# Second feed-forward by seven products of halves, output projection in four chunks of 276 tokens

## The chip, the cores and the metric

One NeuronCore of a Trainium2 chip runs the whole kernel. The metric is the device time of one execution in microseconds (us). TensorE is the engine of matrix products, VectorE and ScalarE work element by element, GpSimd is a slower third one of that kind, and SyncE (SP) issues nearly all DMA transfers.

## What is computed

One layer of a streaming encoder over 1104 tokens (64 of one group, 16 meta tokens and 1024 of the other), model width 1024, inner width 2816, all in float32:

```python
def half_ffn(x, g, wg, wu, wd):
    h = rmsnorm(x, g)
    return x + 0.5 * ((jax.nn.silu(h @ wg) * (h @ wu)) @ wd)
...
        xp = half_ffn(xp, ffn1_norm[l], ffn1_wg[l], ffn1_wu[l], ffn1_wd[l])
...
        xp = xp + jnp.concatenate([gdn_p, mla_p.astype(gdn_p.dtype)], axis=-1) @ w_out[l]
...
        xp = half_ffn(xp, ffn2_norm[l], ffn2_wg[l], ffn2_wu[l], ffn2_wd[l])
...
    y_prompt = rmsnorm(xp[:, N_META:], final_norm)
```

Between the two feed-forwards lie an input projection, gated DeltaNet heads and latent attention heads; their concatenated output goes through `w_out`. The change touches what comes after attention: the output projection, the second feed-forward and the final norm.

## The kernel before

**Products.** Activations lie transposed, features on partitions and tokens along the free axis. Each float32 operand is split into a high part of type fp32r and a low rest (`wh`, `wl` of a weight, `XH`, `XL` or `ih`, `il` of an activation); a product is three passes, high by high, high by low and low by high (`PASSES`, `mm3`). A weight block of 128 rows by 128 columns is held in the array, tokens stream.

**Chunks.** Tokens are cut two ways. `CH` has three chunks of 336, 384 and 384 tokens. The first feed-forward's gate and up products use four chunks of `F` = 276, taken as two pairs.

**First feed-forward (span 24 to some 800 us).** Its gate and up products are made by seven products of halves: of a pair of chunks, one half of the model width each and gate and up of one inner tile, sums and differences are formed (`half_weights`, `third_weights` and `last_weights` for weights, `norm_pair` for activations `s`), multiplied in the order of `STEPS` (P1, P5, P6, P3, P7, P2, P4), each product 4 blocks x 3 passes, and the results added up on VectorE in `sn` tiles. So 84 matmuls do what 96 do plainly. The first `NPL` = 5 inner tiles are made plainly for pair 0 (`plain_steps`), then 17 steps for both pairs, then 5 for pair 1 (`half_steps`). The inner tile `hb` goes to DRAM (`hd`). Then `down` follows as a stage of its own: `inner_loads` brings `hd` back and splits it, `down_loads` loads and splits the weights `wd`, and `down` multiplies two inner tiles at a time for eight row blocks and the three chunks of `CH`.

**Output projection (1456 to 1584 us).** `out_in` loads the attention's output `oT` row block by row block for chunk 0, 1 and 2 of `CH`, `out_split` splits it (odd rows on GpSimd). `out_proj` runs over eight output blocks `m`, first for chunk 0 alone, in part between attention's last matmuls, then for chunks 1 and 2 together, with 8 weight blocks loaded each time. `add_x1` and `after_o` add the residual, `stats` and `norm_chunk` form the norm's factor and the split input of the second feed-forward.

**Second feed-forward (1584 to 2399 us).** `ffn` goes over 22 inner tiles: `gu` multiplies gate and up over all three chunks (8 blocks x 3 passes x 3 chunks each), `silu` and `gated` make the inner tile and split it in SBUF, and `down` for two inner tiles is woven in two tiles later. The last two tiles go chunk by chunk in `order2` = (1, 2, 0), so that the final norm (`resid_final`, `final_chunk`, `final_turn`) of a chunk runs under the next one's products. `final_turn` turns the result back to rows by products with `ident`, and `fy` is the scaled row tile that is stored.

**Order of work.** `Tasks` interleaves generators at build time by a cost model (`Clock`), so each engine's instructions stand in a fixed order in the program; an engine waits in that order. All instructions carry the line of one recording helper (L424), so rows of the trace are told apart by their tile names.

The step of seven products reads:

```python
STEPS = (("P1", "A0", 0, "B"), ("P5", "S0", 3, "D"), ("P6", "S1", 4, "B"), ("P3", "T1", 2, "D"),
         ("P7", "T0", 5, "B"), ("P2", "A1", 1, "E"), ("P4", "B1", 6, "B"))
```

Of the kernel before, what the change touches and what calls it, by code (L numbers as in the profile page):

```python
# [17 lines left out]
P = 128  # L18
# [72 lines left out]
def f32(ap):  # L91
    return ap.bitcast(F32)
# [470 lines left out]
def ffn_weights(wg, wu, wd):  # L563

    v = [w.rearrange("(k p) n -> p k n", p=P) for w in (wg, wu)]
    g, u = [[Weight("w", x[:, :, j * P:(j + 1) * P], 8, P) for j in range(NF)] for x in v]
    d = [Weight("wd", wd[j * P:(j + 1) * P, :].rearrange("p (k n) -> p k n", n=P), 8, P) for j in range(NF)]
    order = [g[0], u[0], g[1], u[1]]
    for j in range(2, NF, 2):
        order += [g[j], u[j], d[j - 2], d[j - 1], g[j + 1], u[j + 1]]  # L570
    return (g, u, d), order + d[-2:]


def ffn(s, X, xs, W, wk, hp, ready, order, after):

    nc, T = s.nc, s.tasks
    V, A = nc.vector, nc.scalar
    wg, wu, wd = W
    sg, hs, fl = {}, {}, Flags()

    def h_tiles(j):
        hs[j] = tuple(hp.tile([P, T_], F32R, tag=t, name=t, bufs=CAPS["h"]) for t in ("hh", "hl"))

    def silu(j, c, b):
        w = CH[c][1]
        yield 0, "sg"
        T.take("sg")
        x = wk.tile([P, 384], F32, tag="sg", name="sg", bufs=CAPS["sg"])
        A.activation(x[:, :w], b[:, :w], AF.Silu)
        T.free("b")  # L590
        sg[j, c] = x

    def gated(j, c, b):
        off, w = CH[c]
        yield 0, "hf", lambda: nc.complete(sg[j, c]) if (j, c) in sg else None
        T.take("hf")
        if j not in hs:
            h_tiles(j)
        f = wk.tile([P, 384], F32, tag="hf", name="hf", bufs=CAPS["hf"])
        h, l = [x[:, off:off + w] for x in hs[j]]  # L600
        V.tensor_tensor(f[:, :w], b[:, :w], sg[j, c][:, :w], ALU.mult)
        T.free("b", "sg")
        A.copy(h, f[:, :w])
        yield
        V.tensor_tensor(l, f[:, :w], f32(h), ALU.subtract)
        T.free("hf")
        fl.add((j, c), nc.complete(*hs[j]))

    def product(w, c, out, j, last):
        yield 0, "b", split_w(nc, w), ready.wait((c, 0))  # L610
        b = grab(s)
        for k in range(8):
            if k:
                yield 0, ready.wait((c, k))
            mm3(nc, b[:, :CH[c][1]], [x[:, k, :] for x in w.w], [x[:, k, :] for x in xs[c]], k == 0, k == 7)
        if last:
            T.free("w")
        T.add(out(j, c, b), -1)

    def passes(bs, ws, movs, first, last):  # L620
        for i, (x, y) in enumerate(PASSES):
            for c in range(3):
                nc.tensor.matmul(bs[c][:, :CH[c][1]], ws[x], movs[c][y], start=(first and i == 0), stop=(last and i == 2))

    def all_chunks(w, out, j):
        yield 0, "b", "b", "b", split_w(nc, w)
        bs = [grab(s) for c in range(3)]
        for k in range(8):
            passes(bs, [x[:, k, :] for x in w.w], [[x[:, k, :] for x in xs[c]] for c in range(3)], k == 0, k == 7)
            if k < 7:  # L630
                yield 0
        T.free("w")
        for c in range(3):
            T.add(out(j, c, bs[c]), -1)

    def gu(j, skip=False):
        if not skip:
            yield from all_chunks(wg[j], silu, j)
        yield 0, "h"
        T.take("h")  # L640
        h_tiles(j)
        yield from all_chunks(wu[j], gated, j)

    def evac(m, bs):
        for c in range(3):
            w = CH[c][1]
            V.scalar_tensor_tensor(X[c][:, m, :], bs[c][:, :w], 0.5, X[c][:, m, :], ALU.mult, ALU.add)
            T.free("b")
            yield 0

    def down(j):
        for m in range(8):
            yield (0, "b", "b", "b", split_w(nc, wd[j]), split_w(nc, wd[j + 1])) + ((fl.wait(*[(i, c) for i in (j, j + 1) for c in range(3)]),) if not m else ())
            bs = [grab(s) for c in range(3)]
            for i in (0, 1):
                passes(bs, [x[:, m, :] for x in wd[j + i].w], [[x[:, o:o + w] for x in hs[j + i]] for o, w in CH], i == 0, i == 1)
                if not i:
                    yield 0
            T.add(evac(m, bs), -1)
        T.free("wd", "wd", "h", "h")  # L660

    T.take("h")
    for c in range(3):
        for i, (w, out, j) in enumerate(((wg[0], silu, 0), (wu[0], gated, 0), (wg[1], silu, 1))):
            T.add(product(w, c, out, j, c == 2), 50 + 3 * c + i)
    yield from gu(1, True)
    for j in range(2, NF, 2):
        yield from gu(j)
        yield from down(j - 2)
        if j < NF - 2:  # L670
            yield from gu(j + 1)
    j = NF - 2
    yield 0, "h"
    T.take("h")
    h_tiles(j + 1)
    for c in order:
        o, w = CH[c]
        yield from product(wg[j + 1], c, silu, j + 1, c == order[-1])
        yield from product(wu[j + 1], c, gated, j + 1, c == order[-1])
        bs = {}  # L680
        for i, m in [(i, m) for i in (0, 1) for m in range(4)] + [(i, m) for m in range(4, 8) for i in (0, 1)]:
            if not i:
                yield 0, "b", split_w(nc, wd[j]), fl.wait((j, c))
                bs[m] = grab(s)
            else:
                yield 0, split_w(nc, wd[j + 1]), fl.wait((j + 1, c))
            mm3(nc, bs[m][:, :w], [x[:, m, :] for x in wd[j + i].w], [x[:, o:o + w] for x in hs[j + i]], i == 0, i == 1)
            if i:
                T.add(after(c, m, bs[m]), -1)
    T.free("wd", "wd", "h", "h")  # L690


F = 276
NPL = 5
# [69 lines left out]
def norm_pair(s, p, ss, src, x, raw, more, gain, wk, waits, ready, spill, free):  # L764
# [9 lines left out]
    for i in (0, 1):  # L774
        c = 2 * p + i
        yield 0, waits(c), ready.wait((0, 6)) if p else lambda: 0.0
        r = wk.tile([P, 3], F32, tag="r3", name="r3", bufs=2)
        rsqrt(s, wk, r, ss[:, 2 * c:2 * c + 3], P, 3, 1.0 / DM, EPS)
# [6 lines left out]
        for gi, (t, lo, hi) in enumerate(pieces(c)):  # L785
            o, n = TT[t]
            nc.tensor.matmul(rb[:, lo - F * c:hi - F * c], s.ones[:n], dg[:n, gi, lo - o:hi - o], start=True, stop=True)
# [38 lines left out]
class Ring:  # L826


    def __init__(self, s, name, tiles):
        self.s, self.name, self.tiles, self.n = s, name, tiles, 0  # L830
        s.tasks.caps[name] = len(tiles)
        s.tasks.idle[name] = [0.0] * len(tiles)
# [5 lines left out]

    def more(self, tile):

        T = self.s.tasks
        self.tiles.append(tile)
        self.n = 1
        T.caps[self.name] += 1
        T.idle[self.name].append(T.clock.at["tensor"])
# [26 lines left out]
def half_weights(s, seq, rings, raw, W):  # L872
# [3 lines left out]

    for e in range(NPL):
        to = rings["TS"[e % 2]]
        yield 0, to.name, nc.when(raw, (e, "rA"))
        for i, n in enumerate("AB"):  # L880
            h, l = (rings["A"] if n == "A" else to).take()
# [11 lines left out]
    for e in range(NPL, len(seq)):  # L893
# [42 lines left out]
def plain_steps(s, js, W, x, ready, tmp, hd, done):  # L936
# [22 lines left out]
    for c, e in [(0, 0), (0, 1), (1, 0), (1, 1)] + [(c, e) for e in range(2, NPL) for c in (0, 1)]:  # L959
# [16 lines left out]
def half_steps(s, seq, W, x, ready, tmp, hd, done, hooks):  # L976
# [1673 lines left out]
```

## Time and profile before

| | |
|---|---|
| median of 3 runs | 2412.79 us (2409.34 to 2413.97) |
| the profiled execution | 2413.15 us, its span 2411.3 us |
| mean granted clock of TensorE | 0.987 |
| TensorE busy | 2347.2 us, 97% of the span, 15570 matmuls |
| VectorE, ScalarE, GpSimd busy | 1335.3 us (55%), 803.5 us (33%), 248.8 us (10%) |
| moved by DMA | 177.06 MB, 73 GB/s on average |

The span is what the profile sees between the first and the last instruction; the time of an execution holds a little around it. Matmuls overlap, so a duration in a row is not what one adds: the count of matmuls in a stretch without idle time is.

### The profile page before, as it was taken

What the parts mean: (1) busy time and instruction counts of PE and PEld (TensorE: products, weight loads), DVE (VectorE), ACT (ScalarE), POOL (GpSimd) and SP (SyncE); (2) the same over time, 40 slices, a digit from 0 to 9 for tenths busy, and PEclk for the clock granted to TensorE, in tenths of its full rate; (3) what the DMA queues carried; (4) which work ended last, traced back from release to release, by engine and by line L of the source; (5) the groups of instructions that cost most, each with busy time, mean ns of one, the idle gap of its engine ahead of it and who ended that gap; (6) DMA issues with size and microseconds to landing.
All of it is one profiled execution on the core that took longest, in us unless ns stands there. A gap on an engine that the chain in (4) does not pass through costs nothing.

```text
span 2411.3 us, 39048 instructions
## 1 busy us (share of the span) xinstructions
PE 2347.2 (97%) x15570; PEld 2320.3 (96%) x15570; DVE 1335.3 (55%) x3156; ACT 803.5 (33%) x1799; POOL 248.8 (10%) x557
## 2 busy tenths in 40 slices
PE   9999999989999999899998999999999999999998
PEld 9999999989999899899998998999999999999998
DVE  7754455566667667788877566543323333323336
ACT  5333333331112454555543555331111111111113
POOL 0000000000000413222354001230000000000002
PEclk9999999999999999999999999999999999999999
DMA  6322222362321231112212014412111111111102
GB/s 195 110 77 82 82 81 71 109 221 87 110 82 52 99 96 38 57 38 61 53 57 85 15 44 144 150 36 62 53 44 44 39 32 53 53 45 44 36 27 75
DMA packets 202629, 177.06 MB, mean 73 GB/s; under 512 B 12628, under 2 KB 183808, under 8 KB 202320
## 3 DMA queue, kind: packets, MB, share of 16 engines
q1 hardware_dynamic: 202432, 174.57, 23.4%
q8 instruction: 122, 2.00, 0.4%
q14 instruction: 59, 0.48, 0.1%
q10 hardware_dynamic: 16, 0.00, 0.0%
HBM read 138.94 MB, written 35.60 MB: 72 GB/s over the span
## 4 chain that ended last, share of the span: by engine, by line
PE 85%; DVE 8%; DMA 2%; issue 2%; ACT 2%; POOL 1%; SPq 0%; DVEq 0%; POOLq 0%; ACTq 0%
PE bk L424 85%; DVE s L424 1%; DVE cv L424 1%; DMA raw<-in_ffn_wu_dram 1%; DVE wl L424 1%; DVE rs_q L424 1%; DVE rs_r L424 0%; POOL rs_q L424 0%; DVE st L424 0%; ACT s L424 0%; DMA raw<-in_ffn_wd_dram 0%; ACT wh L424 0%; POOL XL L424 0%; POOL tkq L424 0%; DMA wx<-in_ffn_wg_dram 0%
## 5 line engine op out<-in xcount | busy, mean ns | idle before, releaser
L424 PE MATMUL bk<-XH,wh 128*128 128x384 f32 (+1 forms) x1264 | 354.3, 341 | 0.0
L424 PE MATMUL bk<-XL,wh 128*128 128x384 f32 (+1 forms) x1264 | 349.1, 337 | 1.4 <-POOL XL L424 0.8
L424 PE MATMUL bk<-XH,wl 128*128 128x384 f32 (+1 forms) x1264 | 348.7, 336 | 0.0
L424 ACT CAST wh<-raw 128x1024 fp32r<-128x1024 f32 (+4 forms) x115 | 108.6, 946 | 610.5 <-PE bk L424 573.0
L424 PE MATMUL bk<-s,wh 128*128 128x276 f32 x1472 | 284.1, 291 | 4.9 <-ACT sn L424 2.2
L424 DVE TENSOR_TENSOR wl<-raw,wh 128x1024 fp32r<-128x1024 f32 (+4 forms) x115 | 127.4, 1109 | 216.5 <-ACT wh L424 216.5
L424 PEld LDWEIGHTS bk<-s,wh 128*128 128x128 f32 x1472 | 232.3, 188 | 6.1 <-ACT sn L424 2.5
L424 PEld LDWEIGHTS bk<-XL,wh 128*128 128x128 f32 x1264 | 225.4, 189 | 3.0 <-POOL XL L424 1.7
L424 PEld LDWEIGHTS bk<-XH,wh 128*128 128x128 f32 x1264 | 225.7, 189 | 0.0
L424 PEld LDWEIGHTS bk<-XH,wl 128*128 128x128 f32 x1264 | 225.3, 189 | 0.0
L424 PE MATMUL bk<-s,wl 128*128 128x276 f32 x736 | 213.2, 290 | 0.2 <-DVE wl L424 0.2
L424 PE MATMUL bk<-s,wx 128*128 128x276 f32 x1476 | 196.6, 290 | 1.8 <-DVE s L424 1.8
L424 PEld LDWEIGHTS bk<-s,wx 128*128 128x128 f32 x1476 | 191.3, 188 | 2.0 <-DVE s L424 2.0
L424 DVE SCALAR_TENSOR_TENSOR X<-bk,X 128x384 f32<-128x384 f32 (+1 forms) x264 | 127.3, 534 | 106.7 <-PE bk L424 106.6
L424 DVE SCALAR_TENSOR_TENSOR R<-bk,R 128x384 f32<-128x384 f32 (+1 forms) x252 | 121.4, 533 | 76.8 <-PE bk L424 76.4
L424 PEld LDWEIGHTS bk<-s,wl 128*128 128x128 f32 x736 | 138.6, 188 | 0.4 <-DVE wl L424 0.4
L424 PE MATMUL bk<-cTh,wh 128*128 128x336 f32 x416 | 134.1, 322 | 0.9 <-ACT cTh L424 0.9
L424 PE MATMUL bk<-cTl,wh 128*128 128x336 f32 x416 | 133.1, 320 | 1.6 <-POOL cTl L424 1.2
L424 PE MATMUL bk<-cTh,wl 128*128 128x336 f32 x416 | 133.0, 320 | 0.0
L424 PE MATMUL bk<-hh,wdh 128*128 128x336 f32 (+1 forms) x528 | 122.6, 330 | 0.0
L424 PE MATMUL bk<-hh,wdl 128*128 128x336 f32 (+1 forms) x528 | 122.0, 329 | 0.0
L424 PE MATMUL bk<-hl,wdh 128*128 128x336 f32 (+1 forms) x528 | 121.8, 329 | 0.0
(418 smaller groups left out, 4530.5 us busy)
## 6 DMA issues: line engine op xcount, KB each, us to landing
raw<-in_ffn_wd_dram SPq DMA_DIRECT2D x42, 512.0 KB, 3.7
raw<-in_ffn_wu_dram SPq DMA_DIRECT2D x52, 256.0 KB, 4.6
wx<-in_ffn_wg_dram SPq DMA_DIRECT2D x25, 512.0 KB, 4.3
hd<-hb SPq DMA_DIRECT2D x44, 276.0 KB, 2.1
raw<-in_ffn_wg_dram SPq DMA_DIRECT2D x22, 512.0 KB
raw<-in_ffn_wu_dram SPq DMA_DIRECT2D x22, 512.0 KB, 3.8
raw<-in_w_in_dram SPq DMA_DIRECT2D x16, 512.0 KB, 4.3
raw<-in_w_out_dram SPq DMA_DIRECT2D x16, 512.0 KB, 4.3
```

What stands on the lines that cost most here:

```text
L424: r = f(*args, **kw)
```

## The change

The plain `ffn` with its loads is gone. The code that ran the first feed-forward's seven products becomes a class `Seven`, used for both. For the second one 4 inner tiles are plain for pair 0, 18 steps are for both pairs and 4 for pair 1: 26 steps, an even number (the first has 27). Its inner tiles go to DRAM and come back, and its residual is written to DRAM (`x02`) and read back for `down`. The final part is kept. The output projection works on the four chunks of 276: chunk 0, chunk 1, then chunks 2 and 3 together, with a table of 14 weight loads (`loads_o`) of which some serve two chunks (`prods_o`); items 8 to 11 lie in tiles of their own. The attention's output and the residual `x1`, which lie in DRAM by the chunks of `CH`, are loaded in pieces. GpSimd no longer takes part in splitting and in the norm there. The core of the difference:

```diff
-def ffn(s, X, xs, W, wk, hp, ready, order, after):
...
+class Seven:
...
+    KINDS = "wwxwywxwywxwywxwywwwxy"
...
+        npl = o.plain
+        self.hd = [s.dram.tile([P, T_], F32, name=f"hd{j}") for j in range(NF)]
+        self.seq = seq = [(j, [0]) for j in range(npl)] + [(j, [0, 1]) for j in range(npl, NF)] + [(j, [1]) for j in range(npl)]
+        self.E = E = len(seq)
...
+    def early(self, xt):
...
+        yield 0, lambda: 0.0 if (E - npl + 1, "S0") in W1 else None
+        T.add(inner_loads(s, self.hd, lambda g: self.pairs(("XH1", "XL1")[g % 2], F32), self.inner_slots, self.done, self.hs), -2)
...
+        for x in "LH":
+            yield 0, lambda: 0.0 if x == "L" and (E - 2, "T1") in W1 else self.flags.get("last step")
...
+    def flow(self):
...
+        yield from plain_steps(s, range(o.plain), self.W1, o.x[0], o.ready, o.wk, self.hd, self.done)
+        self.flags.add("plain")
...
+        yield 0, lambda: 0.0 if 1 in self.Wd else None
...
+        yield from down(s, self.R, self.x4, self.Wd, self.hs, self.freed, before_last, o.after, o.chunks)
...
-        wo = [out_weights(w_out[0]) for i in range(2)]
...
+        loads_o, wo = (0, 1, 2, 3, 4, 5, 6, 7, 0, 1, 2, 3, 4, 5), {}
+        prods_o = [[(i, i < 5) for i in range(8)], [(5, 0), (6, 0), (7, 1), (8, 0), (9, 0), (10, 0), (11, 0), (12, 0)],
+                   [(12, 0), (6, 0), (7, 1), (8, 0), (9, 0), (10, 0), (11, 0), (13, 3)]]
...
+        o2.first, o2.second, o2.ready, o2.w, o2.plain, o2.chunks, o2.after = left, right, n3, (ffn2_wg, ffn2_wu, ffn2_wd), 4, order2, after2
...
+        def load_o(c, slots, raws):
...
+                for i, lo, hi, at in parts(c):
+                    nc.sync.dma_start(t[:, :, lo:hi], s.oT[i][:, 4 * h:4 * h + 4, at:at + hi - lo])
...
+            yield from out_proj(s, (0,), xo, wo, loads_o, prods_o[0], oin, add_x1)
+            yield 0, state.wait("out", *[("o", 0, m) for m in range(8)])
...
+            load_x1(1)
...
+            seven2.append(Seven(s, o2))
...
+            yield from out_proj(s, (1,), xo, wo, loads_o, prods_o[1], oin, add_x1)
...
+            yield from out_proj(s, (2, 3), xo, wo, loads_o, prods_o[2], oin, add_x1)
+            yield from seven2[0].flow()
```

**The DMA queue of SP at the end of attention, before** (`ol` and `XL` belong to the projection's input, `raw<-in_w_out_dram` is one weight item, `X<-x` the residual):

```order
L424 DMA oT_77<-mof 128x128
L424 DMA ol<-oT_75 128x336 x2
L424 DMA oT_77<-mof 128x128
L424 DMA ol<-oT_76 128x384 x2
L424 DMA raw<-in_w_out_dram 128x8x128
L424 DMA ol<-oT_76 128x384 x2
L424 DMA raw<-in_w_out_dram 128x8x128
L424 DMA ol<-oT_76 128x384 x2
L424 DMA raw<-in_w_out_dram 128x8x128
```

The same place after the change (`s` are slots of pair 1's tiles that hold the raw input):

```order
L424 DMA oT_77<-mof 128x128 x2
L424 DMA s_16919<-oT_75 128x4x60
L424 DMA s_16919<-oT_76 128x4x216
L424 DMA s_16922<-oT_75 128x4x60
L424 DMA s_16922<-oT_76 128x4x216
L424 DMA s_16925<-oT_76 128x4x168
L424 DMA s_16925<-oT_77 128x4x108
L424 DMA s_16947<-oT_76 128x4x168
L424 DMA s_16947<-oT_77 128x4x108
L424 DMA X_16414<-in_w_out_dram 128x8x128
L424 DMA raw<-in_w_out_dram 128x8x128
```

Before, a weight item followed every two row blocks of input; now eight loads of input stand in one run ahead of items 4 and 5 (the last two rows).

**The same queue a little later, after the change**, from the end of chunk 0 (`x_146` is the residual's copy `x02` in DRAM, `X_16414` and `st` take chunk 1's residual, `wx_17231` is the second feed-forward's first gate weight, `s_17314` takes item 8):

```order
L424 DMA x_146<-X_16414 128x4x276
L424 DMA X_16414<-x_0_72 128x4x60
L424 DMA X_16414<-x_1_73 128x4x216
L424 DMA st_17201<-x_0_72 128x4x60
L424 DMA st_17201<-x_1_73 128x4x216
L424 DMA wx_17231<-in_ffn_wg_dram 128x8x128
L424 DMA s_17314<-in_w_out_dram 128x8x128
L424 DMA raw<-in_w_out_dram 128x8x128
```

The spill waits for chunk 0's last addition, and item 8 stands behind it and five loads.

**ScalarE where the second feed-forward's steps end and down begins, after the change** (`wh<-r` and `wx<-raw` split down weights, `ih` are the first two inner tiles, `sn` belongs to the last step):

```order
L424 CAST wh<-r_22912 128x1024
L424 ACTIVATE sn<-sn 128x276
L424 COPY sn<-bk 128x276 x3
L424 CAST wh<-r_23003 128x1024
L424 ACTIVATE sn<-sn 128x276
L424 CAST wx_23215<-raw 128x1024
L424 ACTIVATE sn<-sn 128x276
L424 CAST wh<-raw 128x1024
L424 CAST ih<-XH_23059 128x1104 x2
```

In the kernel before, the first feed-forward has at this place, where `st` are the inner tiles:

```order
L424 CAST wh<-r_5235 128x1024
L424 ACTIVATE sn<-sn 128x276
L424 CAST st_5571<-XH_5291 128x1104
L424 CAST wx_5575<-raw 128x1024
L424 ACTIVATE sn<-sn 128x276
L424 CAST st_5571<-XH_5291 128x1104
L424 CAST wh<-raw 128x1024
```

The split of the first inner tile stood ahead of both down weights that come through `raw`; now both stand ahead of it.

## Rows read from the trace of the kernel before

**Rows 1.** The page: busy time by engine (part 1), the chain that ended last (part 4).

```profile
PE 2347.2 (97%) x15570; PEld 2320.3 (96%) x15570; DVE 1335.3 (55%) x3156; ACT 803.5 (33%) x1799; POOL 248.8 (10%) x557
...
PE bk L424 85%; DVE s L424 1%; DVE cv L424 1%; DMA raw<-in_ffn_wu_dram 1%; DVE wl L424 1%; DVE rs_q L424 1%; DVE rs_r L424 0%; POOL rs_q L424 0%; DVE st L424 0%; ACT s L424 0%; DMA raw<-in_ffn_wd_dram 0%; ACT wh L424 0%; POOL XL L424 0%; POOL tkq L424 0%; DMA wx<-in_ffn_wg_dram 0%
```

**Rows 2.** Windows: us; busy (count) of PE, PEld, DVE, ACT, POOL; clock; DMA share; GB/s.

```profile
300.00:450.00 150.00, 150.00 (x1179) 150.00 (x1178) 75.22 (x141) 56.14 (x112) 0.00 (x0) 1.00 0.25 76
1700.00:1800.00 100.00, 100.00 (x597) 100.00 (x596) 32.79 (x53) 19.33 (x32) 0.00 (x0) 1.00 0.18 53
1608.00:2390.00 782.00, 782.00 (x4676) 781.96 (x4676) 278.46 (x500) 134.72 (x225) 15.03 (x12) 1.00 0.15 44
```

**Rows 3.** Groups of PE's instructions by form, 1584.5 to 2399 us: busy, mean ns, idle before.

```profile
L424 PE MATMUL bk<-XH,wh 128*128 128x384 f32 x704 | 187.0, 337 | 0.0
```

**Rows 4.** Windows in the first feed-forward, columns as in rows 2.

```profile
24.10:518.20 494.10, 483.23 (x3776) 481.10 (x3776) 287.11 (x532) 198.71 (x378) 0.00 (x0) 1.00 0.31 96
...
120.00:465.00 345.00, 343.27 (x2694) 343.05 (x2692) 172.00 (x320) 129.21 (x258) 0.00 (x0) 1.00 0.26 79
...
518.20:533.00 14.80, 7.87 (x30) 6.73 (x29) 6.02 (x8) 3.33 (x4) 0.00 (x0) 0.65 0.92 336
...
526.00:533.00 7.00, 5.95 (x19) 5.44 (x20) 4.86 (x7) 1.74 (x2) 0.00 (x0) 0.53 1.00 382
```

**Rows 5.** Windows in the output projection and after it, columns as in rows 2.

```profile
1484.30:1515.95 31.65, 29.37 (x176) 28.49 (x175) 22.35 (x25) 17.17 (x28) 11.98 (x9) 0.95 0.84 254
1515.95:1584.50 68.55, 68.55 (x404) 68.55 (x403) 29.05 (x50) 21.41 (x39) 14.23 (x23) 1.00 0.36 107
...
1584.00:1608.00 24.00, 22.52 (x136) 20.87 (x135) 14.03 (x30) 9.58 (x17) 11.53 (x31) 0.93 0.08 23
```

**Rows 6.** Timeline at the projection's start, SP and PE: start, us, instruction, idle before.

```profile
1486.33 0.80 SPq L424 DMA_DIRECT2D ol<-oT  x2
...
1488.13 0.52 PE L424 MATMUL bk<-cTl,wh 128*128 128x336 f32 x1 [1.24 <-POOL cTl L424]
```

**Rows 7.** The page, DMA issues (part 6): count, KB each, median us to landing.

```profile
raw<-in_w_out_dram SPq DMA_DIRECT2D x16, 512.0 KB, 4.3
```

**Rows 8.** The DMA view of 1140 to 1260 us: packets, then queue 1.

```profile
DMA packets 8239, 6.72 MB, mean 56 GB/s; under 512 B 3000, under 2 KB 8224, under 8 KB 8224
...
q1 hardware_dynamic: 8224, 6.54, 18.5%
```

**Rows 9.** The window of the first 24 us, columns as in rows 2.

```profile
0.00:24.00 24.00, 22.43 (x160) 21.65 (x160) 13.88 (x40) 13.52 (x24) 0.20 (x4) 1.00 0.82 265
```

**Rows 10.** PE's waits, 0 to 520 us: in total, times, longest.

```profile
PE bk L424 <- DVE s L424: 3.6, 4, 1.8
PE bk L424 <- DVE dg L424: 2.3, 1, 2.3
```

**Rows 11.** Timeline of 514 to 534 us: the first feed-forward's seam.

```profile
524.42 1.04 ACT L424 CAST wx<-raw 128x1024 fp32r<-128x1024 f32 x1 [8.60 <-DMA raw<-in_ffn_wd_dram]
...
525.70 1.09 ACT L424 CAST st<-XH 128x1104 fp32r<-128x1104 f32 x1
...
526.85 1.29 PE L424 MATMUL bk<-st,wh 128*128 128x336 f32 x3 [6.67 <-ACT st L424]
```

**Rows 12.** The end: PE's timeline from 2397 us, and DVE's groups, 2388 to 2412 us.

```profile
2396.74 0.31 PE L424 MATMUL bk<-hl,wdh 128*128 128x336 f32 x1
...
2398.27 0.32 PE L424 MATMUL bk<-hh,wdl 128*128 128x336 f32 x1
...
2401.46 2.38 PE L424 MATMUL bk<-ident,XG 128*128 128x128 f32 x20
...
L424 DVE TENSOR_SCALAR fy<-bk,fr 128x512 f32<-128x512 f32 x5 | 3.6, 747 | 3.0 <-PE bk L424 2.9
```

**Rows 13.** Groups of DVE's instructions by form: 120 to 465 us, then 1700 to 1800 us.

```profile
L424 DVE TENSOR_TENSOR sn<-bk,sn 128x276 f32<-128x276 f32 x96 | 42.6, 444 | 84.8 <-PE bk L424 82.9
...
L424 DVE SCALAR_TENSOR_TENSOR X<-bk,X 128x384 f32<-128x384 f32 x16 | 8.1, 547 | 0.0
```

More of the change, by code (lines that the diff above doesn't have):

```diff
@@ L574, in ffn @@
-def ffn(s, X, xs, W, wk, hp, ready, order, after):
[L576 to L690, printed above, removed]
@@ L761, in in_out, with norm_pair @@
     yield
-def norm_pair(s, p, ss, src, x, raw, more, gain, wk, waits, ready, spill, free):
+def norm_pair(s, p, sums, src, x, raw, more, gain, wk, waits, ready, spill, free):
     nc, T = s.nc, s.tasks
@@ L1123, in down @@
     g = NF - 2
-    for c, (o, w) in enumerate(CH):
+    for c in chunks:
+        o, w = CH[c]
         for m in range(8):
@@ L2217, in out_proj @@
+    nc.vector.tensor_tensor(l, o, f32(h), ALU.subtract)
+    ready.add((c, k), nc.complete(l))
+    s.tasks.free("ol", of=o)
+def out_proj(s, cs, xs, ws, blocks, items, ready, evac):
     nc, T = s.nc, s.tasks
-    for m in range(8):
-        yield (0, split_w(nc, ws[m]), cond) + ("b",) * len(cs)
+    for i, freed in items:
+        yield (0, nc.when(ws, i)) + ("b",) * len(cs)
+        m = blocks[i]
         bs = [grab(s) for c in cs]
         for k in range(8):
-            if k:
-                yield 0, ready.wait(*[(c, k) for c in cs])
-            else:
-                yield 0, ready.wait(*[(c, 0) for c in cs])
-            for i, (x, y) in enumerate(PASSES):
+            yield 0, ready.wait(*[(c, k) for c in cs])
+            for n, (x, y) in enumerate(PASSES):
@@ L2307, in layer_kernel @@
         nc.vector.memset(ss, 1.0)
-        x0 = s.dram.tile([8, P, T_], F32, name="x0")
-        hd = [s.dram.tile([P, T_], F32, name=f"hd{j}") for j in range(NF)]
+        o1 = K()
+        o1.go = lambda: 0.0
+        o1.first, o1.second, o1.wx, o1.wk, o1.x, o1.ready, o1.w, o1.plain, o1.chunks = right, left, wx, wk, x01, n1, (ffn1_wg, ffn1_wu, ffn1_wd), 5, range(3)
+        x0 = o1.x0 = s.dram.tile([8, P, T_], F32, name="x0")
         staged = {}
@@ new lines, in add_x1, with squares2 @@
+            if c:
+                yield
+                yield from squares2(c, m)
+        def squares2(c, m):
+            x = X2[c, m // 4][:, m % 4, :]
+            yield "sg" if len(acc2.get(c, ())) < 2 else "nt"
+            if len(acc2.get(c, ())) < 2:
+                T.take("sg")
+                a = o2.wk.tile([P, F], F32, tag="sg", name="acc", bufs=CAPS["sg"])
+                acc2.setdefault(c, []).append(a)
+                nc.scalar.activation(a, x, AF.Square)
+            else:
+                if not T.idle["nt"]:
+                    yield 0, "nt"
+                T.take("nt")
+                q = o2.wk.tile([P, F], F32, tag="nt", name="sq", bufs=CAPS["nt"])
+                nc.scalar.activation(q, x, AF.Square)
+                yield nc.lag(q)
+                a = acc2[c][m % 2]
+                nc.vector.tensor_tensor(a, a, q, ALU.add)
+                T.free("nt", of=q)
+            state.add(("q", c, m))
@@ L2550, in squares0 @@
         def squares0():
-            yield 0, state.wait("out", *[("o", 0, m) for m in range(8)]), "sg", "sg"
-            T.take("sg", "sg")
-            a = [s.fw2.tile([P, 384], F32, tag="sg", name="acc", bufs=CAPS["sg"]) for i in (0, 1)] + [0]
+            yield 0, state.wait("swapped", *[("o", 0, m) for m in range(8)])
             for m in range(8):
-                yield from square(s, 0, m, s.X2[0], a, s.fw2)
-            yield from stats(s, 0, a[:2], s.at["f2"], s.X2[0], s.xs2[0], s.fw2, n3)
+                yield from squares2(0, m)
@@ L2571, in then @@
                 last = c == order2[-1]
[L2572 removed]
+                T.add(final_chunk(s, c, sums[c], fin, bs[c], y_rows, s.fw2, "w", own), -1)
                 if not last:
@@ new lines, in out_splits @@
+        def out_splits():
+            for i, m in enumerate(loads_o):
+                own = 8 <= i < 12
+                yield 0, lambda: nc.complete(raws_o[i][0]) if i in raws_o else None, "wx0" if own else "w"
+                T.take("wx0" if own else "w")
+                if own:
+                    h, l = [o2.x[0].new(k, F32R).rearrange("p k t -> p (k t)")[:, :1024] for k in (3 + m, 10 + m)]
+                else:
+                    h, l = [s.wp.tile([P, 1024], F32R, tag=n, name=n, bufs=3) for n in ("wh", "wl")]
+                r, tag = raws_o[i]
+                nc.scalar.copy(h, r)
+                yield nc.lag(h)
+                nc.vector.tensor_tensor(l, r, f32(h), ALU.subtract)
+                wo[i] = tuple(y.rearrange("p (a n) -> p a n", n=P) for y in (h, l))
+                T.free(tag)
+            state.add("wo")
@@ new lines, in flow2 @@
+            o2.even = even
+            state.add("swapped")
+            T.free("rawx", "rawx", *["wx0"] * 4)
+            seven2.append(Seven(s, o2))
+            for p in (0, 1):
+                T.add(norm_pair(s, p, sums2, lambda c, h: X2[c, h], o2.x[p], lambda: st, None if p else lambda i: s.x2s.new((6, 13)[i], F32R), s.at["f2"], o2.wk,
+                                lambda c, h=None: state.wait(*[("q", c, m) for m in range(8)]) if h is None else state.wait(*[("o", c, m) for m in range(4 * h, 4 * h + 4)]),
+                                n3, lambda c: 0, (lambda: seven2[0].flags.get("plain")) if p else lambda: 0.0), 5 + p)
```

439 lines of the change are left out of this document (254 added, 185 removed).

## The prediction

> **What bounds the kernel now.** The page's own totals come first: TensorE is busy 97% of the 2411.3 us span, and 85% of the chain that ended last is its matmuls into `bk` [rows 1]. So a stage is worth what its matmuls take, plus the stretches in which TensorE stands still, and the reader should look for those two things only. The profiled execution took 2413.15 us, 1.85 us more than its span and 0.36 us above the median of 2412.79; the sum below is made against the span.
>
> The windows give the price of a matmul where TensorE never idles. In the first feed-forward, which already works by seven products at 276 columns, 1179 in 150 us are 0.1272 us each; in the second, at mixed 336 and 384 columns, 597 in 100 us are 0.1675 us each; and from 1608 to 2390 us TensorE is busy 782.00 of 782.00 us [rows 2]. Nothing is to be had there except by issuing less. Per column the two rates are nearly equal (0.1675/368 = 0.455 ns, 0.1272/276 = 0.461 ns), so the gain is in columns, not in the shape.
>
> **The change, part by part.**
>
> *Gate and up products.* Before, 22 inner tiles x 2 matrices x 8 blocks x 3 passes x 3 chunks = 3168 matmuls; the groups of this stage show 704 of a pass at 384 columns [rows 3], two chunks' worth. After, 4 tiles of pair 0 stay plain (2 chunks x 2 x 8 x 3 = 96 each) and the other 40 (tile, pair) units take 7 x 4 x 3 = 84: 384 + 3360 = 3744. 3168 x 0.1675 = 530.6 us become 3744 x 0.1272 = 476.2: **-54.4 us**. The down products keep their number (22 x 8 x 3 x 3 = 1584) and widths.
>
> *The cover of what is added.* Sums of inputs and weights, spills of the inner tiles to DRAM and their reloads are all new here, and gate and up weights of four tiles are read twice. The first feed-forward does the same per step: from 120 to 465 us VectorE is busy 172.00 of 345 us, ScalarE 129.21, the DMA engines 0.26, TensorE 343.27 [rows 4]. A step of both pairs is 168 x 0.1272 = 21.4 us, so some 10.7 us of VectorE lie under it. I cost this at nothing in the steady part; with TensorE's cover gone it would be those 10.7 us per step. GpSimd loses its splits, sums and square roots (14.23 us busy from 1515.95 to 1584.50 us); they go to VectorE and ScalarE, which have 29.05 and 21.41 of 68.55 us busy there [rows 5].
>
> *Output projection, products.* 64 blocks of output by 9 matmuls are 576 in the mixed widths and become 768 at 276: 576 x 0.1675 = 96.5 against 97.7, **+1.2 us**. The ten fewer weight loads free no time of TensorE: the second half of this stage has no idle at all, 68.55 of 68.55 us [rows 5].
>
> *Output projection, waits.* The first half lost 31.65 - 176 x 0.153 (the rate at 336 columns, ten from 2396.74 to 2398.27 [rows 12]) = 4.7 us before: idle, a wait of 1.24 us on a split at its start in it [rows 6], and a granted clock of 0.95, so part of the stretch ran at the lower of its two levels, 1.2 GHz instead of 2.4, which is some 1.6 us [rows 5]. I leave that as it is. New is what stands on SP's queue: eight loads of the attention's output (2.26 MB) ahead of weight items 4 and 5, and chunk 0's spill, 1.13 MB of `x1` and a gate weight ahead of item 8. The first half moved 254 GB/s at a DMA share of 0.84 [rows 5], 302 GB/s if full, so the eight loads take 7.5 us; then item 4 needs its own 4.3 us [rows 7] and two splits of 1.1 us each. SP issued its loads some 2 us before TensorE's last start-up wait ended [rows 6], so item 4 is there 12.0 us after chunk 0 gets going; it is wanted after (4 x 24 - 18) x 0.1272 = 9.9 us: late by 2. Item 8 is wanted 3 x 24 x 0.1272 = 9.2 us after chunk 1 starts, and 2.2 MB (7.2 us), the 4.3 and the 2.2 us make 13.7: late by 4.5. **+6.5 us**, and **+1.5** for a second stretch at the lower clock level like the one above. Bounds: -4.7 (nothing late, the old wait gone too) and +15 (each late by twice as much, and the clock).
>
> The chunk borders cut these loads into runs of 60 to 276 columns. The nearest row for short runs: from 1140 to 1260 us 3000 of 8239 packets were under 512 B, and the queue moved 6.54 MB in 18.5% of 120 us [rows 8], 295 GB/s of full share, against 265/0.82 = 323 in the first 24 us [rows 9]. So I charge nothing more for them. The Trainium skill (DMA: Bandwidth & Descriptors, Specifications) says that transfers below 512 B miss the line rate because of a read-modify-write. By that rule the runs of 60 and 108 columns, 0.69 MB in each of the two bursts, would at half rate make the sum an estimated 4.6 us longer; the trace's 295 against 323 bears out a tenth of such a loss.
>
> *Start of the second feed-forward.* Before, it lost 24 - 22.52 us of idle and, at a clock of 0.93, 1.7 us more: 3.2 us from 1584 to 1608 us [rows 5]. After, it has the first one's start, which from 24.10 to 518.20 us took 494.10 us [rows 4] for 5 x 96 + 39 x 84 = 3756 matmuls, 477.8 us: 16.3 lost. Some of that waits for the input's rows, absent here; the waits of 2.3 us on `dg`, as pair 1's norm falls in, and most of the 3.6 us on the sums `s` remain [rows 10]. I take 8 us: **+4.8**. Bounds: -3.2 and 16.3 - 3.2 = +13.1.
>
> *From gate/up to down.* Before, down is woven into the steps and there is no seam. After, it follows the steps as in the first feed-forward, where 518.20 to 533.00 us hold 30 matmuls (5.0 us at full rate) in 14.80 [rows 4]: 9.8 lost. ScalarE waited 8.60 us for a down weight's DMA; the split `st` that TensorE wanted stood behind it on ScalarE's queue, and TensorE waited 6.67 us [rows 11]; the clock granted from 526 to 533 was 0.53, nearly all at the lower level [rows 4]. In the change the number of steps is even, so the two `XH` loads ahead of that weight can go about a step earlier, but the first split (`ih` now) stands behind two weight splits instead of one. Between 0 and 9.8 I take **+4.5**: the same queue, with less in transfer when it matters.
>
> *The end.* 12.9 us follow the last product before (2398.43 to 2411.3) [rows 12]. In the change 24 of the `ident` turns, 2.8 us (20 took 2.38), fall behind the last product instead of ahead of it, and with them chunk 2's output, six scalings `fy` at 0.75 us [rows 12]: **+3.6** behind, **-2.8** ahead.
>
> **Sum.** -54.4 + 1.2 + 6.5 + 1.5 + 4.8 + 4.5 + 3.6 - 2.8 = -35.1: span 2376.2, execution **2378.0 us**.
>
> **The rivals.**
>
> *Every wait is covered.* If all loads arrive in time, -54.4 + 1.2 + 0.8 = -52.4 stays: 2360.8 us, a few less if the old start-up waits go too. For it: VectorE and ScalarE are half idle [rows 4]. Against it: the one stage that is written this way shows its waits [rows 4, 11].
>
> *Bursts on the DMA.* The seams cost what the rows show at their worst: 15 instead of 8 in the projection, 13.1 instead of 4.8 at the start, 9.8 instead of 4.5 at the end of the steps. Two of three add 12 to 15, 2390 to 2393; all three give 2399. For it: 2.26 MB in one burst where the DMA share is 0.84 already [rows 5]. Against it: two estimates must be off the same way.
>
> *The pace of the steps breaks (slower).* VectorE makes the sums `sn` and those of the weights in each step; if its queue fell behind, every step would wait for it, from the first half step of the second feed-forward on. To end above no change, the 35.1 and 4.8 more (0.2%, about what a measurement of this kernel can tell) must be lost over 18 full and 4 single steps, 20 in all: 2.0 us each, so 23.4 us of VectorE per step where 10.7 are seen [rows 4]. At 2.3 us each the time is 2424. An operation on 276 columns takes 444 ns, one on 384 takes 547 [rows 13], 0.95 ns a column and 0.18 us fixed, and that fixed part is in the 10.7 already. The Trainium skill (VectorE: DVE Perf Modes, The TRN2 errata) has such a fixed cost per instruction and asks for tiles of 512 elements or more; by that rule the many narrower operations are what would make this happen, and the trace agrees that the cost exists.
>
> *The gain is used up.* All three seams at their bounds and an end that loses 6 us or more besides: 2405 to 2417.
>
> **How the numbers follow.** Forecast (2368 to 2390): 0.58. All covered (2357 to 2368): 0.14. Bursts (2390 to 2405): 0.22. Used up: 0.03, half of it within no change. Slower by the pace: 0.03. From these, faster 0.95, same 0.02, slower 0.03. The range 2360 to 2398 leaves out the lowest tail of the second case, the upper third of the third, and the last two: some 0.15.
>
> **What would show it.** Right: steady steps of the second feed-forward at 0.127 us a matmul with no idle; in the projection one wait of 1 to 3 us and one of 3 to 6 us, each on the split of a weight whose DMA landed last; one of 2 to 6 us on `ih` where down begins; 15 to 17 us after the last product. Wrong: idle inside the steady steps, VectorE over 60% there, or a projection that takes over 118 us from attention's last matmul to the first gate product.

## The result and the profile after

| | before | after |
|---|---|---|
| median | 2412.11 us (4 runs) | 2383.67 us (4 runs, 2377.64 to 2387.71) |
| ratio | | 0.9881, 95% interval 0.9856 to 0.9906 |
| profiled execution, span | 2413.15, 2411.3 us | 2385.68, 2383.8 us |
| mean granted clock | 0.987 | 0.982 |
| TensorE busy | 2347.2 us, 15570 matmuls | 2305.1 us, 16356 matmuls |
| VectorE, ScalarE busy | 55%, 33% | 64%, 38% |
| moved by DMA | 177.06 MB | 214.30 MB |

The kernel is 28.4 us faster where 35.1 were forecast. The reader should cut the new profile at the same seams as the sum. Windows of the kernel after, columns as in [rows 2]: chunk 0 of the projection, chunk 1, chunks 2 and 3, the second feed-forward's steps, the steady part of these, the seam, its first 6 us behind, the down products, and what follows the last one:

```profile
1485.36:1515.88 30.52, 25.02 (x178) 23.91 (x177) 19.24 (x26) 14.54 (x20) 0.00 (x0) 0.94 0.73 202
1515.88:1550.01 34.13, 29.68 (x212) 29.13 (x211) 17.00 (x41) 11.02 (x20) 0.00 (x0) 0.90 0.62 172
1550.01:1600.85 50.84, 50.84 (x405) 50.61 (x403) 32.87 (x65) 15.71 (x26) 0.00 (x0) 1.00 0.25 75
1600.85:2086.76 485.91, 481.71 (x3780) 480.60 (x3780) 269.16 (x503) 188.54 (x362) 0.00 (x0) 1.00 0.31 92
...
1620.00:2060.00 440.00, 440.00 (x3463) 440.00 (x3462) 237.57 (x437) 169.20 (x328) 0.00 (x0) 1.00 0.27 82
...
2086.76:2094.02 7.26, 0.00 (x1) 0.00 (x0) 2.61 (x3) 3.49 (x5) 0.00 (x0) 0.65 1.00 405
...
2094.00:2100.00 6.00, 5.80 (x20) 5.29 (x21) 2.92 (x4) 2.03 (x2) 0.00 (x0) 0.57 1.03 411
...
2094.02:2368.08 274.06, 273.88 (x1634) 273.30 (x1635) 185.67 (x339) 56.02 (x73) 14.00 (x12) 0.99 0.25 86
2368.08:2383.80 15.72, 8.03 (x73) 7.67 (x70) 9.02 (x29) 5.01 (x9) 0.00 (x0) 0.85 0.51 183
```

From 1620 to 2060 us TensorE has no idle, 3463 matmuls in 440.00 us are 0.1271 us each, and VectorE is at 54%. That is the gain. What is lost stands in the other lines: the two projection chunks at a clock of 0.94 and 0.90, and the seam, 7.26 us with no matmul and 0.57 behind it.

TensorE's waits in the kernel after, from 1486 us to chunk 0's end, in chunks 1 to 3, and from there to the down products (in total, times, longest; `bk` is the bank that a product is written to, `s` holds inputs or sums of halves, in the projection also weight items):

```profile
PE bk L424 <- ACT wh L424: 3.5, 2, 3.0
PE bk L424 <- DVE wl L424: 2.0, 3, 0.7
...
PE bk L424 <- ACT s L424: 4.0, 1, 4.0
PE bk L424 <- DVE s L424: 0.4, 1, 0.4
...
PE bk L424 <- ACT ih L424: 7.3, 1, 7.3
PE bk L424 <- DVE wl L424: 1.7, 2, 1.4
PE bk L424 <- DVE XH L424: 1.4, 1, 1.4
PE bk L424 <- DVE dg L424: 1.1, 1, 1.1
```

Each of the three large waits is where the forecast put it: on the split of weight item 4, of item 8 (whose tile is a slot `s`), and of the first inner tile `ih`. The timeline of the seam (start, us, engine, instruction, idle before) says what `ih` waited for:

```profile
2080.82 1.58 SPq L424 DMA_DIRECT2D XH<-x  x2
...
2082.45 0.42 SPq L424 DMA_DIRECT2D raw<-in_ffn_wd_dram  x1
...
2085.26 2.29 SPq L424 DMA_DIRECT2D R<-x  x4
...
2090.22 1.04 ACT L424 CAST wx<-raw 128x1024 fp32r<-128x1024 f32 x1 [7.02 <-DMA raw<-in_ffn_wd_dram]
...
2092.86 2.12 ACT L424 CAST ih<-XH 128x1104 fp32r<-128x1104 f32 x2
...
2094.02 1.29 PE L424 MATMUL bk<-ih,wh 128*128 128x336 f32 x3 [7.26 <-ACT ih L424]
```

The loads of the first two inner tiles from `hd` were issued before all this, the last at 2080.40. The third down weight, wanted only some 24 us later (144 matmuls at 0.1675 us), was issued at 2082.45 and split at 2090.22, and the split `ih` stood behind it. It is the picture of [rows 11], with one weight more ahead.

### The profile page after: what moved, and what is told of

Read it like the earlier page. It is cut to its first block, busy times and chain, and to the rows that moved or that the text cites. A ratio compares the mean times of both kernels' runs of the same rounds, so it can differ in the third digit from the quotient of the medians.

```text
span 2383.8 us, 41602 instructions
## 1 busy us (share of the span) xinstructions
PE 2305.1 (97%) x16356; PEld 2277.2 (96%) x16356; DVE 1514.0 (64%) x3531; ACT 908.1 (38%) x1990; POOL 204.4 (9%) x488
## 2 busy tenths in 40 slices
DMA packets 231044, 214.30 MB, mean 90 GB/s; under 512 B 18372, under 2 KB 202864, under 8 KB 230848
## 4 chain that ended last, share of the span: by engine, by line
PE 84%; DVE 9%; DMA 3%; ACT 2%; issue 1%; POOL 1%; SPq 0%; DVEq 0%; POOLq 0%; ACTq 0%
PE bk L424 84%; DVE s L424 1%; DVE cv L424 1%; DVE wl L424 1%; DVE rs_q L424 1%; DMA X<-in_w_out_dram 1%; DVE rs_r L424 0%; POOL rs_q L424 0%; DMA R<-x 0%; ACT s L424 0%; DMA s<-in_w_out_dram 0%; ACT wh L424 0%; DVE st L424 0%; DMA raw<-in_ffn_wd_dram 0%; DMA wx<-in_ffn_wg_dram 0%
## 5 line engine op out<-in xcount | busy, mean ns | idle before, releaser
L424 PE MATMUL bk<-s,wh 128*128 128x276 f32 x3136 | 601.0, 290 | 4.9 <-ACT sn L424 2.2
L424 PEld LDWEIGHTS bk<-s,wh 128*128 128x128 f32 x3136 | 493.0, 188 | 6.3 <-ACT sn L424 2.5
L424 PE MATMUL bk<-s,wl 128*128 128x276 f32 x1568 | 449.4, 290 | 1.9 <-DVE wl L424 1.9
L424 PE MATMUL bk<-s,wx 128*128 128x276 f32 x2964 | 393.9, 290 | 1.6 <-DVE s L424 1.6
L424 PEld LDWEIGHTS bk<-s,wx 128*128 128x128 f32 x2964 | 383.5, 188 | 1.8 <-DVE s L424 1.8
L424 DVE SCALAR_TENSOR_TENSOR R<-bk,R 128x384 f32<-128x384 f32 (+1 forms) x504 | 242.5, 533 | 154.3 <-PE bk L424 153.5
L424 PEld LDWEIGHTS bk<-s,wl 128*128 128x128 f32 x1568 | 293.3, 188 | 2.6 <-DVE wl L424 2.6
L424 PE MATMUL bk<-XH,wh 128*128 128x384 f32 (+1 forms) x576 | 166.6, 343 | 0.0
L424 PE MATMUL bk<-XL,wh 128*128 128x384 f32 (+1 forms) x576 | 161.2, 334 | 0.0
L424 PE MATMUL bk<-XH,wl 128*128 128x384 f32 (+1 forms) x576 | 161.1, 334 | 0.0
L424 DVE TENSOR_TENSOR wl<-wx,wh 128x512 fp32r<-128x512 f32 (+1 forms) x89 | 87.1, 979 | 12.7 <-ACT wh L424 12.7
```

The lines of the kernel that those rows point to most:

```text
L424: r = f(*args, **kw)
```

## The experiments

Every ratio is to the kernel before, measured on the same chip; the change alone has 0.9881 (0.9856 to 0.9906). Not all runs were made on one chip, so ratios are compared, not times. Edits of waits are conditions in the generators: they move instructions in the static order, and nothing of the computation, except in the runs with 138 columns and with eight products.

**The seam, first try.** In both feed-forwards the first two inner tiles are split before the third down weight is waited for:

```diff
+        if j == n:
+            yield 0, lambda: 0.0 if 1 in hs else None
...
-        if g + 1 < NF // 2:
+        if 0 < g < NF // 2 - 1:
...
+        if not g:
+            yield from load(1)
```

> Only the seam from gate/up to down is edited, in both feed-forwards: the first two inner tiles are split on ScalarE before the third down weight is waited for, and the load of the next two inner tiles is issued behind that. Theory (order on ScalarE's queue): the 7.3 us wait on ih in the second feed-forward and the 5.6 us wait on st in the first shrink to under 1.5 us each, the clock stays near 1.00 there, some 9.5 and 8 us go, so about 2366 us against 2383.7 of the change. Rival (the burst of DMA has to be through anyway): TensorE waits as long a few us later, for another inner tile, a down weight or the residual R; the time stays within 2376 to 2384.

Measured: 2374.80 us, ratio 0.9825 (0.9811 to 0.984). The wait on `ih` is gone. TensorE's waits of this run from 2070 to 2120 us:

```profile
PE bk L424 <- ACT sn L424: 2.6, 1, 2.6
PE bk L424 <- DVE XH L424: 1.4, 1, 1.4
PE bk L424 <- DVE R L424: 0.8, 1, 0.8
```

So a good part of it was order; but the split now stood inside the last step and waited there 3.61 us for its own load, and that step's sums `sn` waited behind it, at 3.2 us on `hb` (the inner tile) in the first feed-forward likewise. Less was won than expected.

**The seam, second try**: the same, with the split behind the second down weight's.

```diff
+        if not g:
+            yield 0, lambda: 0.0 if 1 in W else None
```

> The seam again, with the first two inner tiles split on ScalarE behind the second down weight instead of in the middle of the last step's sums (in both feed-forwards). Theory (order on ScalarE's queue): the waits that the first try left there, 2.6 us on sn and 0.8 on R in the second feed-forward, 3.2 on hb and 1.6 on R in the first, fall to under 1 us each on sn and hb; the ratio to the kernel before is 0.980 to 0.982, against 0.9825 of the first try and 0.9881 of the change. Rival (the spilled inner tile itself lands last): a wait of 3 us or more on ih or st, ratio 0.983 or more.

Measured: 2377.70 us, 0.9845 (0.983 to 0.986), not better than the first try: a miss for the theory as it was put, and the rival's wait on `ih` or `st` is not there either. The waits on `sn` and `hb` went, but waits on R (the running sum of the down products with the residual) of 3.9 us came here and of 4.8 us in the first feed-forward. TensorE's waits of this run from 2070 to 2120 us, then VectorE's from 2080 to 2102 us:

```profile
PE bk L424 <- DVE R L424: 3.9, 2, 2.0
...
DVE wx L424 <- ACT wx L424: 6.8, 2, 4.2
DVE sn L424 <- PE bk L424: 4.1, 2, 3.1
```

The late weights block VectorE now: the low parts `wx` of the third and the fifth are waited for (2.7 and 4.2 us), with the additions into R behind them, and TensorE waits for the banks that these free.

**The seam, third try.** On top of the second try the late transfer itself is moved: the third and fourth down weights are loaded ahead of the inner tiles, two residual tiles behind them.

```diff
+    for j in (n, n + 1):
+        yield from load(j)
...
+    yield 0, lambda: 0.0 if len(wd2) > 3 else None
...
-            yield 0, lambda: 0.0 if x == "L" and (E - 2, "T1") in W1 else self.flags.get("last step")
+            yield 0, lambda: (0.0 if (E - 2, "T1") in W1 else None) if x == "L" else 0.0 if 1 in self.hs else None
```

> The seam a third time, in both feed-forwards: the third and fourth down weights are loaded ahead of the first spilled inner tiles, and two of the four residual tiles behind these; the first two inner tiles are split behind the second down weight. Theory (a late transfer at the head of an in-order queue: last time VectorE waited for the third down weight with the additions into R behind it): no wait of over 1.5 us is left at either seam and the clock stays near 1.00, ratio to the kernel before 0.979 to 0.982. Rival (the bytes of the seam have to be through): waits on R or ih of 4 us or more in all remain in the second feed-forward, ratio 0.9825 to 0.985.

Measured: 2368.85 us, 0.9799 (0.9777 to 0.9821). TensorE's waits in the second feed-forward's seam (2070 to 2120 us) and the first's (514 to 545 us), and the window at the seam:

```profile
PE bk L424 <- DVE ih L424: 0.6, 1, 0.6
...
PE bk L424 <- ACT st L424: 0.8, 1, 0.8
PE bk L424 <- DVE st L424: 0.6, 1, 0.6
```

```profile
2081.50:2087.50 6.00, 5.86 (x36) 5.54 (x35) 5.59 (x9) 1.78 (x2) 0.00 (x0) 1.00 0.82 278
```

36 matmuls in 6 us at a clock of 1.00, where the change had 20 in 6 us at 0.57, at its lower level (1.2 GHz) for most of it. The theory held, and the rival's waits on R or `ih` are gone. This is the fastest version, faster than both kernels; its interval lies below that of the change.

**Items 4 and 5 early.** Their loads go between chunk 1's and chunk 2's input.

```diff
             yield from load_o(1, (6, 13), raws)
+            yield 0, lambda: 0.0 if 5 in raws_o else None
             yield from load_o(2, (5, 7), raws)
```

> Only the SP queue is edited: weight items 4 and 5 of the output projection are issued behind chunk 1's four loads of the attention's output instead of behind all eight. Theory (place in the queue): the waits of 2.98 and 0.74 us in chunk 0 are under 0.5 us in all, and the stretch at the lower clock behind them goes too, some 5 us less: about 2379. Rival (the DMA engines are full, so what is moved ahead pushes something else out): a new wait of 3 to 5 us on chunk 1's or chunk 2's input s, time 2382 to 2386.

Measured: 2388.57 us, 0.9873 (0.9857 to 0.9889), no difference to the change. Neither was right: the wait on item 4 grew, from 2.98 to 4.45 us, as ScalarE had the split of chunk 2's input, which now came later, ahead of item 4's.

**The same with the splits in order**, `yield 0, lambda: 0.0 if 5 in wo else None` ahead of `split_o(2, raws)`.

> As the try with items 4 and 5 early on SP, and on ScalarE their splits now stand ahead of the split of chunk 2's input, which had waited 5.49 us for its DMA with item 4 behind it. Theory (the head of an in-order queue, not bandwidth): the waits in chunk 0 fall from 4.45 and 1.42 us to under 1 us in all, ratio 0.985 to 0.9865. Rival (the DMA engines are full until 1503 us): the weights themselves land late, the wait stays at 3 us or more, ratio 0.987 or more.

Measured: 2385.47 us, 0.9872 (0.9852 to 0.9892). The rival held, though for another item. TensorE's and then ScalarE's waits from 1486 to 1516 us, and the window of 1490 to 1506 us:

```profile
PE bk L424 <- ACT wh L424: 4.3, 1, 4.3
PE bk L424 <- DVE wl L424: 2.5, 3, 1.4
...
ACT s L424 <- DMA s<-oT: 5.3, 6, 2.6
ACT wh L424 <- DMA X<-in_w_out_dram: 4.2, 2, 2.6
ACT wh L424 <- DMA raw<-in_w_out_dram: 1.2, 2, 0.7
...
1490.00:1506.00 16.00, 11.59 (x90) 11.14 (x88) 11.89 (x18) 8.61 (x13) 0.00 (x0) 1.00 1.09 297
```

Item 4 was in time within 1.4 us, and item 6, issued behind six loads of input and a spill, was then 4.3 us late. From 1490 to 1506 us the DMA engines are full (a share of 1.09, 297 GB/s), so here bytes count: what is moved ahead sets something else back.

**Item 8 early**: items 8 to 11 ahead of chunk 1's residual and the gate weight.

```diff
-            load_x1(1)
+            def x1_later():
+                yield 0, lambda: 0.0 if 9 in raws_o else None
+                load_x1(1)
+                state.add("x1 in")
+                seven2.append(Seven(s, o2))
```

> Only the SP queue is edited: weight items 8 to 11 are issued ahead of chunk 1's residual and of the second feed-forward's first gate weight. Theory (place in the queue): the 4.45 us wait in chunk 1 falls under 1.5 us and the lower clock behind it goes, 5 to 7 us less: about 2378. Rival: the additions of chunk 1 then wait for the residual, TensorE waits for a free PSUM bank or for the sums of chunk 1's norm, as long as before; time 2382 to 2388.

Measured: 2402.41 us, 0.9933 (0.9918 to 0.9948), slower than the change. Waits of all engines from 1516 to 1550 us:

```profile
DVE st L424 <- DMA st<-x: 14.7, 1, 14.7
...
PE bk L424 <- DVE s L424: 8.1, 1, 8.1
```

The additions of the residual stood on VectorE ahead of item 8's low part; loading the residual later made VectorE wait 14.7 us for it, and TensorE 8.1 us for item 8. A second loss lies at the start of the steps, 7.56 us in two pieces, and it was there in three other runs too (below).

**Halves of the residual.** The half that the first additions need is loaded ahead of items 8 to 11, the other behind.

> Half of chunk 1's residual (the half that the first additions need) is loaded ahead of items 8 to 11, the other half and the first gate weight behind them. Theory (VectorE waited for the residual with item 8's split behind it): the 4.45 us wait in chunk 1 falls to under 2.5 us, and no new one of over 2 us comes up before the steps; ratio 0.985 to 0.987. Rival: with the gate weight and the second half late, a wait of 3 us or more on the sums of the norm or on the first gate product takes its place, ratio 0.988 or more.

Measured: 2395.01 us, 0.9918 (0.9903 to 0.9933). Within chunk 1 the theory held: 0.8 us on `acc` (the norm's sums) and 1.2 on `wl` are left of 4.4. But at 1599 us TensorE waits for the split of the first gate weight (a row of its waits from 1516 to 1600 us):

```profile
PE bk L424 <- ACT wh L424: 2.9, 1, 2.9
```

That is the place and about the size that the rival named, and the 7.56 us at the start of the steps come on top; the two cost more than was won.

**All three first tries together.**

> The three edits together. Theory: the three seams are independent, the savings add: 17.5 + 5 + 6 us, about 2355. Rival (a shared limit, the DMA engines): the sum comes to less than half, 2369 or more.

Measured: 2395.88 us, 0.9909 (0.9894 to 0.9924): the waits on item 8 (8.1 us), item 4 (4.2 us) and at the start of the steps (7.56 us) ate what the seam gave. It says nothing on a shared limit.

**Runs of 138 columns.**

```diff
+def even_parts(c):
+    return [(c, 0, 138, 0), (c, 138, F, 138)] if c in (1, 2) else parts(c)
```

> The change, but the pieces of 60 and 216, and of 168 and 108, columns are cut into two of 138 each (552 bytes), with the same number of loads and bytes; chunks 1 and 2 read their attention output and residual at other columns, so the output differs. Theory (short runs cost nothing that counts): the waits of 2.98 and 0.74 us in chunk 0 and 4.45 us in chunk 1 stay within 0.7 us, ratio 0.987 to 0.9895. Rival (runs under 512 bytes go at half rate): each burst is 2 us shorter, the three waits fall by 3 us or more together, ratio 0.9865 or less.

Measured: 2389.54 us, 0.9887 (0.987 to 0.9904), no difference. The DMA view of the burst, ten microseconds each, of the change (1488 to 1498 us) and then of this run (1487 to 1497 us):

```profile
DMA packets 5456, 2.99 MB, mean 299 GB/s; under 512 B 1845, under 2 KB 5455, under 8 KB 5455
```

```profile
DMA packets 5632, 2.99 MB, mean 299 GB/s; under 512 B 145, under 2 KB 5631, under 8 KB 5631
```

A third of the packets under 512 B, or hardly any: 299 GB/s either way, and the three waits stay within 0.2 us (3.10, 0.74 and 4.60). The rule of the Trainium skill that the prediction weighed (DMA: Bandwidth & Descriptors, Specifications) would have had the first slower; this row does not show it.

This run also had the 7.56 us at the start of the steps, though it edits nothing there. TensorE's timeline of it:

```profile
1619.73 0.83 PE L424 MATMUL bk<-s,wh 128*128 128x276 f32 x2 [4.92 <-ACT wh L424]
...
1623.21 0.60 PE L424 MATMUL bk<-s,wl 128*128 128x276 f32 x1 [2.64 <-DVE wl L424]
```

ScalarE's order there, of the change and then of this run:

```order
L424 ACTIVATE sg<-bk 128x276
L424 CAST wh<-raw 128x512 x2
L424 ACTIVATE sg<-bk 128x276
L424 CAST s_18254<-X_16414 128x1104
L424 CAST s_18275<-X_16414 128x1104
```

```order
L424 ACTIVATE sg<-bk 128x276 x2
L424 CAST s_18248<-X_16414 128x1104
L424 CAST s_18256<-X_16414 128x1104
L424 CAST wh<-raw 128x512 x2
```

The build's planner had turned the weights of the second plain step and pair 1's input round. All four runs with the weights behind have the 7.56 us, and none of the others.

**Item 8 by halves, with that order held.** The gate weight is early again, and the split of pair 1's input waits for the second step's weights.

```diff
+                    return lambda: g() if not p or (1, "B") in seven2[0].W1 else None
```

> As the try with the halves of chunk 1's residual, the first gate weight loaded as early as in the change, and on ScalarE the split of the second plain step's weights is put ahead of the split of pair 1's input. Theory (the 7.56 us wait of four earlier tries is the order on ScalarE, not the edit that each was made for): no wait of over 2 us in the first 30 us of the second feed-forward, chunk 1's wait under 2.5 us, ratio 0.985 to 0.987 against 0.9881 of the change. Rival (the loads of the residual are what is late): the 7.56 us wait or one like it is still there, ratio 0.990 or more.

Measured: 2385.80 us, 0.9877 (0.9851 to 0.9902). The 7.56 us are gone, as the order on ScalarE would have it, and chunk 1 waits 3.0 us in four pieces. But at 1600 us a wait of 3.0 us on the first gate weight's split stands, as in the run with the halves, that the change does not have, so nothing is left of the gain. With the weight loaded early the wait is as long as with it late, so the late load was not its cause: on ScalarE the split stands behind squares for the norm, which wait for VectorE's sums (2.91 and 0.93 us).

**All of it**: the third seam, this one, and items 4 to 7 ahead of the input of chunks 2 and 3.

> Both of these and, for chunk 0, weight items 4 to 7 loaded ahead of the input of chunks 2 and 3. Theory: the seams of the change cost some 30 us of waits and lower clock, and most of it can be had by order alone: ratio 0.974 to 0.979, about 2355 us. Rival (what is won at one place is waited for at the next): ratio 0.981 or more.

Measured: 2369.96 us, 0.9803 (0.9783 to 0.9823), the same as the seam alone. TensorE's waits from 1478 to 1600 us:

```profile
PE bk L424 <- DVE wl L424: 5.2, 5, 1.5
PE bk L424 <- ACT wh L424: 3.0, 1, 3.0
PE bk L424 <- DVE s L424: 2.5, 3, 1.5
PE bk L424 <- DVE acc L424: 0.8, 1, 0.8
```

The ratio lies between the theory's and the rival's. But for one of 3.0 us, the gate weight's, the large waits have become small ones, and in all they are no less: 11.5 us, where the change has 11.6 over the same work (1486 to 1612 us). The times do not tell this version and the seam alone apart. So in the projection it went as the rival had it: what is won at one place is waited for at the next.

**Eight products instead of seven**, in the second feed-forward; P4 is multiplied twice, with no other work added.

```diff
+                for r in range(1 + (name == "P4" and npl == 4)):
```

> The change with one of the seven products of the second feed-forward multiplied twice, so 96 matmuls per tile and pair instead of 84 (its result is added twice, so the output differs). Theory (TensorE's matmul count sets the time of the steps): 40 x 12 x 0.1272 = 61 us more, 2440 to 2448 us, ratio 1.010 to 1.016, steps of 24.4 us without idle. Rival (the steps are paced by VectorE, ScalarE or the loads and have slack on TensorE): less than 45 us more, ratio under 1.007, with idle in the steps of the change.

Measured: 2446.55 us, 1.012 (1.0095 to 1.0145). The ratio is 0.0239 above that of the change, some 58 us; 61 were expected from TensorE's count. Its steady window, then the steps from the first wait on a gate weight's low part to the last matmul, of the change and of this run:

```profile
1660.00:2060.00 400.00, 400.00 (x3153) 400.00 (x3152) 178.26 (x330) 130.32 (x267) 0.00 (x0) 1.00 0.23 69
...
1602.80:2086.76 483.96, 481.19 (x3778) 480.30 (x3778) 267.21 (x499) 188.54 (x362) 0.00 (x0) 1.00 0.30 91
...
1603.07:2145.60 542.53, 541.36 (x4258) 540.68 (x4258) 267.32 (x499) 185.21 (x362) 0.00 (x0) 1.00 0.27 82
```

480 more matmuls take 58.6 us more. So the steps have no slack, and an eighth product costs about what its matmuls take. It is the other side of the -54.4 us. At the seam behind them TensorE waits 10.7 us for `ih` in this run instead of 7.3, which is no part of the steps.

## Why the prediction was right

*Gate and up products, -54.4.* Right. The steady rate is 0.1271 us where 0.1272 was taken, without idle, and the run with eight products shows that the count sets it.

*The cover.* Right: VectorE 54% and ScalarE 38% of the steady window, against 50% and 37% in [rows 4]. The rival that VectorE paces the steps is out, and with it the end that was slower.

*Output projection.* From attention's last matmul to the first gate product it took 115.5 us, within the 118 named. Products right: chunks 2 and 3 take 50.84 us for 405 matmuls without idle. The two waits are at their places, item 4's at 3.7 us instead of 2 and item 8's at 4.4 instead of 4.5. What was too small is the clock: 0.94 and 0.90 over 30.52 and 34.13 us are 1.8 and 3.4 us, of which 1.6 had been left in the first half and 1.5 added. In all 30.52 + 34.13 - (178 + 212) x 0.1272 = 15.0 us are lost where 4.7 + 6.5 + 1.5 = 12.7 were taken. The prediction's side estimate of 4.6 us for short runs, which is not in the sum, took 0.69 MB of them for each burst; the second has only the runs of 60 columns, 0.25 MB, so it should have been 3.1.

*Start, 8 us.* 485.91 - 3780 x 0.1272 = 5.1 us were lost: too high by 3.

*The seam, 4.5.* This is the step that was mis-sized. 7.26 us of wait and some 2.6 of clock (0.57 over 6 us) make 9.8, as much as the upper bound of 9.8 from [rows 4], and 5.3 more than taken; the wait lies outside the 2 to 6 us that were named as its sign. The reason given for less, "the two `XH` loads ahead of that weight can go about a step earlier", failed: they went out at 2080.82, 5.9 us before the steps ended, against 4.8 in the first feed-forward of the kernel before (515.35 and 520.18): one microsecond earlier, not a step. The other one given, two weights ahead of the first split, was the right one: the first edit of that order took 0.56% off the time, and moving the late transfer 0.8%, in two seams.

*The end.* 15.7 us instead of 16.5.

Seam +5.3, projection +2.3, start -2.9 and end -0.8 give +3.9 of the 7.6 us between the span of 2376.2 and 2383.8; the rest lies in small pieces that were not followed. That the total came no further off is in part luck, as the start, taken too high, makes up for half of the seam's error.

*The rivals.* "Every wait is covered" is out, by the three waits. "Bursts on the DMA" has one seam at its bound and the others not, and 2383.67 us lies in the stretch given to the forecast itself. What the runs add is that two of the waits are not made by the burst alone: at the seam what stood ahead on ScalarE and VectorE counts too, and in chunk 1 the order of the loads (4.4 us became 3.0), while in chunk 0 the DMA engines are full and order only moved the wait.

## What to carry to other kernels

Where TensorE is busy all the time, count matmuls at the measured rate for their width; the count is the gain, and all the rest of a forecast is the seams. At a seam, follow each in-order queue for a first instruction whose transfer lands last and is wanted last: moving a load only on the issuing queue is half an edit, as the instruction that waits for it stands at its old place on the other engines. When a planner sets the order, compare the orders of two builds at every seam before a difference in time is laid to the edit.

## What was not expected

Issuing a transfer can take long when many stand ahead of it. In the change the eight loads of chunk 1's and 2's input held SP's queue for 5.37 us, and the second weight load behind them took 2.33:

```profile
1486.35 5.37 SPq L424 DMA_DIRECT2D s<-oT  x8
...
1492.97 2.33 SPq L424 DMA_DIRECT2D raw<-in_w_out_dram  x1
```

In the kernel before, where weight and input loads take turns, the same load took 0.38 us:

```profile
1487.34 0.38 SPq L424 DMA_DIRECT2D raw<-in_w_out_dram  x1
```

In the run with the splits in order six loads held the queue for 7.48 us, and item 6 stood behind them. That a queue of issues falls back to the pace of the data once a burst is long enough is a reading of these rows; no run tests it.

And the seam edits give more than the idle time that they remove, since the stretch behind the wait ran at the lower clock: at the seam 2.6 us behind 7.26.
